# The moving operands of the dense products begin 96 bytes past a multiple of 128 in their partition

## The chip, the cores and the metric

The program runs on one core of one Trainium2 chip. A time is the time that the device takes for one execution, in microseconds (us). The kernel before takes 1717.57 us, the median of 3 runs (1716.57 to 1721.44). The profile was taken in an execution of its own.

## The reference

Two transformer-like blocks on 256 tokens of 1024 channels, all in float32. The first block: a parallel mixer (forgetting attention beside a causal convolution of width 31), cross attention to a memory of 256 tokens, and a mixture of 32 experts. The second block has two layers, each with two feed-forward networks (FFNs) and a mixer between them.

```python
def swiglu(h, w13, w2):
    gate, up = jnp.split(h @ w13, 2, axis=-1)      # 1024 -> 2 x 2816
    return (jax.nn.silu(gate) * up) @ w2           # 2816 -> 1024

for l in range(2):
    if l == 1:
        k_shared, v_shared = shared_kv(x, kv_norm, w_kv, k_norm)
    x = x + 0.5 * swiglu(rms_norm(x, ffn1_norm[l]), ffn1_w13[l], ffn1_w2[l])
    h = rms_norm(x, mix_norm[l])
    x = x + (rglru_block(h, ...) if l == 0 else stick_breaking_block(h, k_shared, v_shared, ...))
    x = x + 0.5 * swiglu(rms_norm(x, ffn2_norm[l]), ffn2_w13[l], ffn2_w2[l])
```

The four FFNs are the greater part of the time outside the experts.

## The kernel before, in words

**The dense products.** Activations lie with channels on the 128 partitions and the 256 tokens along the free dimension. Float32 accuracy comes from splitting each operand into a high and a low part of type fp32r and adding three matmuls (`mm3`, lines 177 to 179): w-high by x-high (L177), w-high by x-low (L178), w-low by x-high (L179). In each, the 128 x 128 slice of a weight tile `wh` or `wl` is loaded into the array (the stationary operand), and a 128 x 256 slice of an activation tile is streamed through it (the moving operand). The activation tiles are

- `xgh`, `xgl`: the input of a stage, 8 chunks of 256 tokens, read by `proj2` (line 195) in 2 x 8 x 3 = 48 matmuls for each weight tile;
- `hh`, `hl`: one hidden pair of an FFN, 2 chunks, two buffers, read by `rowproj` in 8 x 2 x 3 = 48 matmuls for each weight tile;
- `qT`/`kT` and `zp`/`v` (the mixer's output product), `cath`/`catl` (the memory attention's), `yh`/`yl` (the recurrent block's), `xkvh`/`xkvl` (the stick-breaking block's), read in the same way.

In `product` (line 1174) the roles are turned round: the weights stream, and `xg`, `xkv` or `cat` slices are loaded.

**An FFN** (`ffn`, line 1059) has 11 steps j. Each computes a gate block (48 matmuls into PSUM tile `A`), an up block (48 into `B`), and, from j = 1 to 9, a step of the second product for the pair before (48 matmuls into `acc`). Two pairs are left for the tail, 96 matmuls in which the two weight tiles alternate. Each block takes one weight tile of 1 MB, which a DMA loads, ACT rounds to `wh` (L157) and DVE subtracts to `wl` (L158); three `wh`/`wl` slots rotate.

**Places in memory.** Every pool hands out its tiles one after another in the order of their first request, each rounded up to 32 bytes. Where a tile begins in its partition is therefore decided by what was requested before it. The pool `x` holds `xgh` and `xgl` and nothing else; `first`, `moe` and `second` follow it and take turns in the same space; `rglru` and `attn` lie behind `second`.

**The experts** (from 257 us to 710 us) read float32 weights by DMA into `raw`, `wh`, `wl` and `xgh`/`xgl`, used there as a ring of 16 buffers, and multiply them without splitting (L941, L967).

Of the kernel before, what the change touches and what calls it, by code (L numbers as in the profile page):

```python
# [8 lines left out]
F32 = mybir.dt.float32  # L9
F32R = mybir.dt.float32r  # L10
I32 = mybir.dt.int32
# [5 lines left out]
P = 128  # L17
T = 256
# [29 lines left out]
class Block:  # L48
    def __init__(s, ctx, tc, io):
        s.tc, s.nc, s.ctx, s.io = tc, tc.nc, ctx, io  # L50
        s.n = s.turn = s.place = 0
        s.queue = None
        pool = lambda name, bufs, **k: ctx.enter_context(tc.tile_pool(name=name, bufs=bufs, **k))
        s.cp = pool("const", 1)
        s.wp = pool("weights", 3)
        s.tp = pool("temps", 2)
        s.xp = pool("x", 1)
        s.pa = pool("acc", 1, space=PSUM)
        s.pp = pool("ps", 2, space=PSUM)

# [32 lines left out]
    def col(s, name, c=0, n=1):  # L93
        o = PCOL[name] + c
        return s.par[:, o:o + n]

    def pair(s, pool, C, tag, bufs=None, N=T):
        return (s.new(pool, [P, C, N], tag + "h", F32R, bufs), s.new(pool, [P, C, N], tag + "l", F32R, bufs))
# [126 lines left out]
    def rsqrt(s, x, n):  # L225

        nc = s.nc
        xh = s.tmp([P, n], f"nr{n}", 6 if n > 4 else 8)
        nc.vector.tensor_scalar_mul(xh, x, -0.5)
        yi = s.tmp([P, n], f"nr{n}", 6 if n > 4 else 8).bitcast(I32)  # L230
        nc.vector.tensor_single_scalar(yi, x.bitcast(I32), 1, op=ALU.arith_shift_right)
        y = s.tmp([P, n], f"nr{n}", 6 if n > 4 else 8)
        nc.vector.tensor_scalar(y.bitcast(I32), yi, -1.0, float(0x5F3759DF), op0=ALU.mult, op1=ALU.add)
        u = s.tmp([P, n], f"nr{n}", 6 if n > 4 else 8)
        for _ in range(3):
            if n == 2:
                for i in range(n):
                    c = slice(i, i + 1)
                    nc.vector.scalar_tensor_tensor(u[:, c], y[:, c], xh[:, c], y[:, c], op0=ALU.mult, op1=ALU.mult)
            else:  # L240
                nc.vector.tensor_mul(u, y, y)
                nc.vector.tensor_mul(u, u, xh)
            nc.vector.scalar_tensor_tensor(y, u, 1.5, y, op0=ALU.add, op1=ALU.mult)
        return y
# [779 lines left out]
    def after_moe(s, acc, p2):  # L1024


        nc = s.nc
        gg = s.new(p2, [P, KC], "gg")
        nc.vector.tensor_mul(gg, s.col("final_g", 0, 8), s.col("ffn1_norm_2", 0, 8))

        g2 = s.tmp([P, 2 * KC], "nr16", 6).rearrange("p (k n) -> p k n", n=2)
        nc.vector.memset(g2, 1.0)
        nc.vector.tensor_mul(g2[:, :, 1], s.col("final_g", 0, 8), s.col("final_g", 0, 8))
        xg = s.pair(s.xp, KC, "xg")
        st = s.sums_pe(g2)
        for b in range(4):
            s.update(acc[b], b, 1.0, xg, gg, st)
        got = {}

        def rows(what):  # L1040
            if not got:


                x = s.tmp([P, 4], "nr4", 8)
                pb = s.bank()[0]
                nc.vector.tensor_scalar_mul(x.rearrange("p (n h) -> p n h", h=2), st["pe"].rearrange("p h n -> p n h"), 1.0 / D)
                nc.vector.tensor_scalar_add(x[:, 0:2], x[:, 0:2], EPS)
                nc.vector.scalar_tensor_tensor(x[:, 2:4], x[:, 0:2], EPS, x[:, 2:4], op0=ALU.mult, op1=ALU.add)
                y = s.rsqrt(x, 4)
                got["r"] = s.spread(y[:, 2:4], pb)  # L1050
                got["r1"] = s.spread(y[:, 0:2], pb, s.tmp([P, T]))
            return got[what]

        def rescale():
            for k in range(KC):
                nc.vector.scalar_tensor_tensor(s.xT[:, k], s.xT[:, k], s.col("final_g", k), rows("r1"), op0=ALU.mult, op1=ALU.mult)
        return xg, rows, rescale

    def ffn(s, pf, xg, rows, w13, w2, g, extra=None, between=None):

        nc = s.nc
        J = F // 256
        step, tail = s.rowproj(w2, 2 * J)
        held = []
        for j in range(J):
            pg, pu = s.ps([P, 2, T], "A"), s.ps([P, 2, T], "B")
            w = s.wload(w13[j], KC, 256)
            s.proj2(pg, w, xg, late=2 if j == 0 else 0)
            w = s.wload(w13[J + j], KC, 256)
            s.proj2(pu, w, xg)  # L1070
            rb2 = bc(rows("r"), [P, 2, T], 1)
            tg, tu = s.tmp([P, 2, T], "gs", 2), s.tmp([P, 2, T], "us", 2)
            nc.vector.tensor_mul(tg, pg, rb2)
            nc.scalar.activation(tg, tg, AF.Silu)
            nc.vector.tensor_mul(tu, pu, rb2)
            nc.vector.tensor_mul(tu, tu, tg)
            hl = s.pair(pf, 2, "h", 2)
            s.split(hl, slice(0, 2), tu)
            held.append((j, hl))
            if 0 < j < J - 1:  # L1080
                step(*held.pop(0))
            if j == 4 and between is not None:
                between()
        if g is None:
            outv = s.io["out"].rearrange("(c p) t -> p c t", p=P)

            def done(ps, b):
                s.update(ps, b, 0.5, None, None, None)
                nc.sync.dma_start(outv[:, 2 * b:2 * b + 2], s.xT[:, 2 * b:2 * b + 2])
            tail(held, done)  # L1090
            return None
        xg, st, done = s.residual(0.5, g)

        def done2(ps, b):
            done(ps, b)
            if extra is not None:
                for m in (2 * b, 2 * b + 1):
                    s.split(extra[0], m, s.xT[:, m], extra[1][:, m:m + 1])
        tail(held, done2)
        return xg, s.rows(st)  # L1100

    def rglru(s, pr, xg, rows, g):
# [7 lines left out]
        def branch(col, dst, late=0):  # L1110
            w = s.wload(io["a_w_in_2"][col // 256], KC, 256)
            ps = s.ps([P, 2, T])
            s.proj2(ps, w, xg, late=late)
            nc.vector.tensor_mul(dst, ps, bc(rows("r"), [P, 2, T], 1))
# [186 lines left out]
    def run(s):  # L1301
        tc, io = s.tc, s.io
        s.setup()
        with tc.tile_pool(name="first", bufs=1) as p1:
            s.cur = p1
            xg, rows, km, vm = s.mixer(p1)
            xg, st = s.mem_attention(p1, xg, rows, km, vm)
        with tc.tile_pool(name="moe", bufs=1) as mt:
            acc = s.moe(mt, xg, st)
        with tc.tile_pool(name="second", bufs=1) as p2:  # L1310
            s.cur = p2
            xg, rows, rescale = s.after_moe(acc, p2)
            gains = lambda name, l: s.col(name, 8 * l, 8)
            ffn = lambda xg, rows, n, l, g, *more: s.ffn(
                p2, xg, rows, io[f"ffn{n}_w13_2"][l], io[f"ffn{n}_w2_2"][l], g, *more)
            xg, rows = ffn(xg, rows, 1, 0, gains("mix_norm_2", 0), None, rescale)
            with tc.tile_pool(name="rglru", bufs=1) as pr:
                xg, rows = s.rglru(pr, xg, rows, gains("ffn2_norm_2", 0))
            with tc.tile_pool(name="attn", bufs=1) as pk:
                xkv = s.pair(pk, KC, "xkv")  # L1320
                xg, rows = ffn(xg, rows, 2, 0, gains("ffn1_norm_2", 1), (xkv, gains("kv_norm_2", 0)))
                kT, vA = s.shared_kv(pk, xkv, rows)
                xg, rows = ffn(xg, rows, 1, 1, gains("mix_norm_2", 1))
                xg, rows = s.stick(pk, xg, rows, kT, vA, gains("ffn2_norm_2", 1))
            ffn(xg, rows, 2, 1, None)
# [76 lines left out]
```

## Time and profile before

| | |
|---|---|
| median of 3 runs | 1717.57 us |
| the profiled execution | 1718.19 us, of it 1716.4 us span |
| TensorE matmul busy (PE) | 1659.7 us, 97% of the span |
| weight loads (PEld) | 1349.5 us, beside the matmuls |
| VectorE (DVE), ScalarE (ACT) | 922.9 us, 704.0 us |
| TensorE clock granted | 0.984 of full speed in the mean |
| DMA | 408.03 MB |

PE is TensorE, "x" is a count of instructions, and L177 is a line of the kernel. Matmuls are pipelined: one is shown with some 280 ns, but in a dense stretch the next begins some 115 ns after it. How fast the stream runs is therefore read from starts: the start of one block of 48 less the start of the block before it, divided by 48.

### The profile page before, as it was taken

Reading aid. Unit: us, or ns where it says so; the run is one execution under the profiler, and the core shown is the slowest. Engines: PE = TensorE matmul, PEld = TensorE weight load, DVE = VectorE, ACT = ScalarE, POOL = GpSimd, SP = SyncE. Lnnn points to the kernel's source line nnn. Section 1 sums busy time; section 2 is a strip of 40 time slices with the busy share of each in tenths; the row PEclk is TensorE's granted clock in tenths of the full one; section 3 lists DMA queues with packets and bytes.
Section 4 is the critical chain, followed back from the end, with each engine's and each line's share of the span. In section 5 each row is a group of like instructions: output and inputs, shape, how many; then the busy total and the mean of one; then the engine's idle time right before and its main releaser. Section 6 shows DMA issues by size and latency. Waiting matters only on the chain.

```text
span 1716.4 us, 28131 instructions
## 1 busy us (share of the span) xinstructions
PE 1659.7 (97%) x11883; PEld 1349.5 (79%) x11883; DVE 922.9 (54%) x1618; ACT 704.0 (41%) x1138; POOL 5.0 (0%) x19
## 2 busy tenths in 40 slices
PE   8999989999999998699999999999999999999998
PEld 7878984444444443299999999999899997689998
DVE  7998741111111110265657886556755558876554
ACT  8526532111111111244445754445644446764442
POOL 0000000000000000000000000000000000000000
PEclk9999989999999999889999999999999999899999
DMA  9334359999999999845553555554555454044530
GB/s 367 132 120 175 142 226 367 419 419 420 419 419 419 420 419 420 361 183 191 197 184 136 197 221 172 197 184 161 198 196 197 174 195 172 25 148 172 197 123 26
DMA packets 60227, 408.03 MB, mean 238 GB/s; under 512 B 6592, under 2 KB 9920, under 8 KB 11456
## 3 DMA queue, kind: packets, MB, share of 16 engines
q1 hardware_dynamic: 60096, 406.18, 61.4%
q8 instruction: 95, 1.56, 0.4%
q14 instruction: 36, 0.29, 0.0%
HBM read 405.11 MB, written 1.05 MB: 237 GB/s over the span
## 4 chain that ended last, share of the span: by engine, by line
PE 54%; DVE 2%; ACT 1%; issue 1%; DMA 0%; SPq 0%; ACTq 0%; DVEq 0%
PE A L179 6%; PE A L178 6%; PE A L177 6%; PE acc L177 5%; PE acc L178 5%; PE B L177 5%; PE B L178 5%; PE acc L179 5%; PE B L179 5%; ACT wh L157 1%; PE A L1262 1%; DVE wl L158 1%; PE A L967 1%; PE B L416 0%; PE B L408 0%
## 5 line engine op out<-in xcount | busy, mean ns | idle before, releaser
L157 ACT CAST wh<-raw 128x1024 fp32r<-128x1024 f32 (+2 forms) x378 | 378.0, 1034 | 445.0 <-issue 363.8
L158 DVE TENSOR_TENSOR wl<-raw,wh 128x1024 fp32r<-128x1024 f32 (+2 forms) x378 | 448.6, 1204 | 160.5 <-ACT wh L157 159.7
L177 PE MATMUL B<-xgh,wh 128*128 128x256 f32 x872 | 246.1, 282 | 6.9 <-ACT wh L157 6.9
L177 PE MATMUL A<-xgh,wh 128*128 128x256 f32 (+1 forms) x872 | 246.7, 283 | 0.0
L179 PE MATMUL A<-xgh,wl 128*128 128x256 f32 (+1 forms) x872 | 245.5, 282 | 0.1
L178 PE MATMUL A<-xgl,wh 128*128 128x256 f32 (+1 forms) x872 | 245.5, 282 | 0.1
L179 PE MATMUL B<-xgh,wl 128*128 128x256 f32 x872 | 245.6, 282 | 0.0
L178 PE MATMUL B<-xgl,wh 128*128 128x256 f32 x872 | 245.2, 281 | 0.0
L178 PE MATMUL acc<-hl,wh 128*128 128x256 f32 x704 | 194.7, 278 | 0.2
L179 PE MATMUL acc<-hh,wl 128*128 128x256 f32 x704 | 194.5, 277 | 0.0
L177 PE MATMUL acc<-hh,wh 128*128 128x256 f32 x704 | 193.1, 278 | 0.5 <-ACT hh L218 0.5
L177 PEld LDWEIGHTS B<-xgh,wh 128*128 128x128 f32 x872 | 164.5, 189 | 7.9 <-ACT wh L157 7.2
L179 PEld LDWEIGHTS B<-xgh,wl 128*128 128x128 f32 x872 | 164.4, 189 | 1.5 <-DVE wl L158 1.0
L178 PEld LDWEIGHTS A<-xgl,wh 128*128 128x128 f32 (+1 forms) x872 | 164.7, 189 | 0.6 <-DVE xgl L222 0.4
L177 PEld LDWEIGHTS A<-xgh,wh 128*128 128x128 f32 (+1 forms) x872 | 164.8, 189 | 0.3
L179 PEld LDWEIGHTS A<-xgh,wl 128*128 128x128 f32 (+1 forms) x872 | 164.7, 189 | 0.4 <-DVE wl L158 0.3
L178 PEld LDWEIGHTS B<-xgl,wh 128*128 128x128 f32 x872 | 164.7, 189 | 0.5 <-DVE xgl L222 0.2
L852 DVE COPY gx<-B 128x128 f32<-128x128 f32 x64 | 18.6, 291 | 231.9 <-PE B L846 223.6
L941 PE MATMUL A<-raw,gx 128*64 128x512 f32 x560 | 130.1, 603 | 8.6 <-DMA raw<-in_w_gu_dram 6.2
L178 PEld LDWEIGHTS acc<-hl,wh 128*128 128x128 f32 x704 | 132.1, 188 | 0.6 <-DVE hl L219 0.6
L179 PEld LDWEIGHTS acc<-hh,wl 128*128 128x128 f32 x704 | 132.2, 188 | 0.0
L177 PEld LDWEIGHTS acc<-hh,wh 128*128 128x128 f32 x704 | 130.9, 188 | 1.2 <-ACT hh L218 1.1
(407 smaller groups left out, 2422.4 us busy)
## 6 DMA issues: line engine op xcount, KB each, us to landing
raw<-in_ffn_w_dram SPq DMA_DIRECT2D x132, 1024.0 KB, 4.8
raw<-in_w_gu_dram SPq DMA_DIRECT2D x70, 1024.0 KB, 19.9
raw<-in_w_down_dram SPq DMA_DIRECT2D x34, 1024.0 KB, 19.9
wh<-in_w_gu_dram SPq DMA_DIRECT2D x22, 1024.0 KB, 19.9
wl<-in_w_gu_dram SPq DMA_DIRECT2D x22, 1024.0 KB, 19.9
wh<-in_w_down_dram SPq DMA_DIRECT2D x11, 1024.0 KB, 19.9
wl<-in_w_down_dram SPq DMA_DIRECT2D x11, 1024.0 KB, 19.9
raw<-in_a_w_in_dram SPq DMA_DIRECT2D x8, 1024.0 KB, 5.0
```

Source lines behind the costliest of these rows:

```text
L157: nc.scalar.copy(wh[:, lo:hi], raw[:, lo:hi])
L158: nc.vector.tensor_sub(wl[:, lo:hi], raw[:, lo:hi], wh[:, lo:hi].bitcast(F32))
L177: mm(out, w[0], x[0], start=first, stop=False)
L178: mm(out, w[0], x[1], start=False, stop=False)
L179: mm(out, w[1], x[0], start=False, stop=last)
L852: nc.vector.tensor_copy(dst, pg[:, :, i])
L941: s.pe(s.nc.tensor.matmul(ps[g * CAP:(g + 1) * CAP], gx[t // 2][:, 2 * (t % 2) + c], w[:, g, c * 512:c * 512 + 512], start=t + c == 0, sto ...
L967: s.pe(nc.tensor.matmul(pd[n * CAP:(n + 1) * CAP], hx[:, 2 * t + c], w[:, c, n * 512:n * 512 + 512], start=t + c == 0, stop=t + c == 2))
L1262: mm(sc[:, lo:lo + ke], qT[b:b + 64, c, qb * P:qb * P + P], kT[b:b + 64, c, 0:ke], start=True, stop=True)
```

## The change

A tile of 32 bytes (`pad`) is requested in the pool `x` ahead of `xgh`. A new helper `lay` requests tiles by tag and size ahead of their use, so that they get the first places of a pool: the mixer's and the memory attention's product tiles in `first`, `hh` and `hl` in `second`, `yh` and `yl` in `rglru`. A tile `pad` of 64 bytes stands behind `hl`, and the buffers `nr4` (16 bytes each, asked for only by the norm behind the experts) are 5 in place of 8, so that what follows comes to 96 as well.

```diff
@@ Block.__init__
         s.xp = pool("x", 1)
+        s.new(s.xp, [P, 8], "pad")
@@ Block
+    def lay(s, pool, *tiles):
+        for tag, n, bufs in tiles:
+            for _ in range(bufs):
+                s.new(pool, [P, n // 4], tag, F32, bufs)
@@ rsqrt (four such lines) and after_moe (one)
-        xh = s.tmp([P, n], f"nr{n}", 6 if n > 4 else 8)
+        xh = s.tmp([P, n], f"nr{n}", 6 if n > 4 else 5 if n == 4 else 8)
...
-                x = s.tmp([P, 4], "nr4", 8)
+                x = s.tmp([P, 4], "nr4", 5)
@@ run
+            s.lay(p1, ("cath", 8192, 1), ("catl", 8192, 1), ("v", 4096, 1), ("qT", 4096, 1), ("kT", 4096, 1), ("zp", 4 * (30 + T) * 4, 1))
             xg, rows, km, vm = s.mixer(p1)
...
+            s.lay(p2, ("hh", 2048, 2), ("hl", 2048, 2), ("pad", 64, 1))
             xg, rows, rescale = s.after_moe(acc, p2)
...
+                s.lay(pr, ("yh", 8192, 1), ("yl", 8192, 1))
                 xg, rows = s.rglru(pr, xg, rows, gains("ffn2_norm_2", 0))
```

The built programs hold the same instructions on every engine, in the same order and with the same waits on the same semaphore values; what differs is where tiles begin. In bytes from the start of the partition:

| tile | before | past 128 | after | past 128 |
|---|---|---|---|---|
| `xgh`, `xgl` | 138816, 147008 | 64 | 138848, 147040 | 96 |
| `hh` (two), `hl` (two) | 163680, 165728, 167776, 169824 | 96 | 155232, 157280, 159328, 161376 | 96 |
| `xkvh`, `xkvl` | 171872, 180064 | 96 | the same | 96 |
| `yh`, `yl` of the recurrent block | 212928, 221120 | 64 | 171872, 180064 | 96 |
| `cath`, `catl` | 172064, 219712 | 32, 64 | 155232, 163424 | 96 |
| `qT`, `kT`, `v`, `zp` of the mixer | 195136, 199232, 186944, 155200 | 64 | 175712, 179808, 171616, 183904 | 96 |
| `wh` (three), `wl` (three) | 77344 to 93728, 101920 to 118304 | 32 | the same | 32 |
| `raw` (eight) | 11808 to 69152 | 32 | the same | 32 |
| expert tiles (`oh`, `gx`, `oT`, `hx`, ...) | | 0 | each 32 further | 32 |

The slices of all these tiles that a dense product reads begin at multiples of 512 bytes from the tile's start, so each has its tile's place past 128.

## Rows read from the trace of the kernel before

**Rows 1.** The page's part 1, TensorE's and VectorE's busy time.
```profile
PE 1659.7 (97%) x11883; PEld 1349.5 (79%) x11883; DVE 922.9 (54%) x1618; ACT 704.0 (41%) x1138; POOL 5.0 (0%) x19
```

**Rows 2.** Windows: the mixer, the four FFNs with their neighbours, and experts.
```profile
core 0: us, PE busy (x) PEld busy (x) DVE busy (x) ACT busy (x) POOL busy (x), PEclk, DMA share, GB/s
30.00:170.00 140.00, 136.42 (x839) 117.28 (x838) 125.22 (x306) 70.83 (x136) 1.83 (x2) 1.00 0.45 169
742.00:930.00 188.00, 187.84 (x1593) 187.35 (x1593) 116.26 (x151) 80.32 (x101) 0.00 (x0) 0.99 0.46 163
1010.00:1200.00 190.00, 189.59 (x1613) 188.05 (x1612) 120.81 (x154) 88.78 (x115) 0.00 (x0) 1.00 0.52 183
1243.00:1433.00 190.00, 189.84 (x1613) 188.64 (x1612) 114.02 (x129) 85.55 (x109) 0.96 (x3) 1.00 0.52 183
1523.00:1716.00 193.00, 188.61 (x1599) 187.36 (x1597) 113.73 (x141) 79.80 (x99) 0.00 (x0) 1.00 0.37 132
400.00:560.00 160.00, 158.52 (x930) 71.70 (x928) 26.19 (x66) 28.99 (x71) 0.00 (x0) 1.00 1.01 419
```

**Rows 3.** Groups of TensorE by shape: busy us, mean ns, idle before.
```profile
L177 PE MATMUL A<-xgh,wh 128*128 128x256 f32 x864 | 244.4, 283 | 0.0
...
L178 PE MATMUL acc<-hl,wh 128*128 128x256 f32 x704 | 194.7, 278 | 0.2
```

**Rows 4.** Timeline of TensorE, first FFN: the first matmul of seven blocks.
```profile
start us, us, engine line op out<-in xcount [idle before <-releaser]
...
765.59 0.28 PE L177 MATMUL acc<-hh,wh 128*128 128x256 f32 x1
...
771.24 0.28 PE L177 MATMUL A<-xgh,wh 128*128 128x256 f32 x1
...
777.00 0.28 PE L177 MATMUL B<-xgh,wh 128*128 128x256 f32 x1
...
782.76 0.28 PE L177 MATMUL acc<-hh,wh 128*128 128x256 f32 x1
...
788.20 0.28 PE L177 MATMUL A<-xgh,wh 128*128 128x256 f32 x1
...
793.81 0.28 PE L177 MATMUL B<-xgh,wh 128*128 128x256 f32 x1
...
799.41 0.28 PE L177 MATMUL acc<-hh,wh 128*128 128x256 f32 x1
```

**Rows 5.** Timeline of TensorE, fourth FFN: the first matmul of four blocks.
```profile
1582.27 0.28 PE L177 MATMUL acc<-hh,wh 128*128 128x256 f32 x1
...
1587.93 0.28 PE L177 MATMUL A<-xgh,wh 128*128 128x256 f32 x1
...
1593.53 0.28 PE L177 MATMUL B<-xgh,wh 128*128 128x256 f32 x1
...
1599.13 0.28 PE L177 MATMUL acc<-hh,wh 128*128 128x256 f32 x1
```

**Rows 6.** Timeline of TensorE, the first FFN's tail and one later wait.
```profile
915.99 0.28 PE L177 MATMUL acc<-hh,wh 128*128 128x256 f32 x1
...
918.25 0.28 PE L179 MATMUL acc<-hh,wl 128*128 128x256 f32 x1
918.69 0.73 PE L177 MATMUL acc<-hh,wh 128*128 128x256 f32 x4 [0.16 <-ACT hh L218]
919.26 0.28 PE L178 MATMUL acc<-hl,wh 128*128 128x256 f32 x1
...
927.63 0.28 PE L177 MATMUL B<-xgh,wh 128*128 128x256 f32 x1
...
1549.27 0.28 PE L179 MATMUL acc<-hh,wl 128*128 128x256 f32 x1
...
1554.34 0.28 PE L178 MATMUL A<-xgl,wh 128*128 128x256 f32 x1
```

**Rows 7.** Timeline of TensorE, the recurrent block's output product, first matmul and its successor.
```profile
987.54 0.28 PE L177 MATMUL acc<-yh,wh 128*128 128x256 f32 x1
...
1010.33 0.28 PE L177 MATMUL A<-xgh,wh 128*128 128x256 f32 x1
```

More of the change, by code (lines that the diff above doesn't have):

```diff
@@ L227, in rsqrt @@
         nc = s.nc
-        xh = s.tmp([P, n], f"nr{n}", 6 if n > 4 else 8)
+        xh = s.tmp([P, n], f"nr{n}", 6 if n > 4 else 5 if n == 4 else 8)
         nc.vector.tensor_scalar_mul(xh, x, -0.5)
-        yi = s.tmp([P, n], f"nr{n}", 6 if n > 4 else 8).bitcast(I32)
+        yi = s.tmp([P, n], f"nr{n}", 6 if n > 4 else 5 if n == 4 else 8).bitcast(I32)
         nc.vector.tensor_single_scalar(yi, x.bitcast(I32), 1, op=ALU.arith_shift_right)
-        y = s.tmp([P, n], f"nr{n}", 6 if n > 4 else 8)
+        y = s.tmp([P, n], f"nr{n}", 6 if n > 4 else 5 if n == 4 else 8)
         nc.vector.tensor_scalar(y.bitcast(I32), yi, -1.0, float(0x5F3759DF), op0=ALU.mult, op1=ALU.add)
-        u = s.tmp([P, n], f"nr{n}", 6 if n > 4 else 8)
+        u = s.tmp([P, n], f"nr{n}", 6 if n > 4 else 5 if n == 4 else 8)
         for _ in range(3):
```

## The prediction

> **What bounds the kernel now.** I read the page's busy times first: TensorE is busy for 97% of the span, VectorE for 54% [rows 1]. Then the windows: in the four FFN stretches PE is busy for 187.84 of 188, 189.59 of 190, 189.84 of 190 and 188.61 of 193 us at full clock, while DVE and ACT have a third of their time left and the DMA queues half of theirs [rows 2]. Nothing is to be seen there but TensorE's own pace. In the experts the DMA engines are full (share 1.01, 419 GB/s), so that stage goes by bytes [rows 2]. The change moves no instruction and no wait; what it can alter is how long one matmul takes, and it tells on the end wherever PE is the bound.
>
> So the pace of the stream is what has to be read. The groups of PE already show a difference: matmuls on `xg` have a mean of 283 ns, those on `hh`/`hl` 278 ns [rows 3]. Since these overlap, I take the timeline and divide blocks of 48 by their starts.
>
> - `hh` block, 782.76 to 788.20: 5.44 us, 113.3 ns a matmul [rows 4].
> - `xg` blocks, 788.20 to 793.81 and to 799.41: 5.61 and 5.60 us, 116.8 ns [rows 4].
>
> `hh` begins 96 past 128 and `xg` 64 past. That is the case for the change. But the same rows hold two things against it. The `hh` block of 765.59 to 771.24 takes 5.65 us, 117.7 ns, on the same tiles [rows 4], and in the fourth FFN the `hh` block from 1582.27 to 1587.93 takes 5.66 us, with its `xg` blocks at 5.60 [rows 5]. So 96 has two paces, 113.3 and 117.8 ns, and each holds through a whole block. Of the 36 step blocks of the four FFNs, 24 run at 113.3 (8 in each of the first three FFNs) and 12 at 117.8 (the first step of each of the three, and all nine of the fourth); one block at 113.3 and two at 117.8 stand in the rows [rows 4, 5].
>
> **When 96 is quick.** The tail of the first FFN shows it within one product. From 915.99 to 918.25 its first 20 matmuls follow the `xg` blocks without a gap: 2.26 / 20 = 113 ns. Then PE waits for ACT (0.16 us), and from 919.26 to 927.63 the other 71 take 8.37 / 71 = 117.9 ns, on the same tiles and weight slots, to the end [rows 6]. I find 15 stretches on tiles at 96 that begin behind a wait or gap, in the tails, the stick-breaking block and the first steps; their means are 117.5 to 118 ns, and 116.8 for one of five matmuls. The first is that tail and the next to last is the first step of the fourth FFN, 1549.27 to 1554.34, 43 matmuls in 5.07 us, 117.9 ns [rows 6]. The quick pace was entered only straight from an `xg` block at 64, and once lost it did not come back within a block. The pace is thus a state that the stream carries with it, and a wait puts it into the slow one.
>
> **The change part by part.** It removes and adds no instruction. Its terms are the streams that change place, and the neighbours that had their pace from them. With every moving tile at 96, no stream at 64 is left from which the quick pace is entered. Each FFN begins with waits for its weights and norms, so I take the slow pace, 5.655 us a block (5.65 and 5.66 measured), as the likeliest for all of them.
>
> 1. `hh` steps that are quick now: 24 x (5.655 - 5.44) = +5.2 us; the first 20 matmuls of three tails: 3 x 20 x 4.5 ns = +0.3 us.
> 2. `xg` blocks of the FFNs, 4 x 22 = 88. Some 78 run at 5.605 now: +0.05 each, +3.9 us. Four run at 5.76 (771.24 to 777.00 and to 782.76 [rows 4], and the two at the same place of the third FFN): -0.1 each, -0.4 us. Some six in first steps run at 5.65 already: 0. Together +3.5 us.
> 3. `xg` blocks of the other stages, 20 of them: +0.05 each, +1.0; in the mixer PE is idle for 3.6 of 140 us and DVE is busy for 125 [rows 2], so part of that is hidden. I take +0.7 us; without any cover it is 1.0.
> 4. `yh`/`yl`: 192 matmuls from 987.54 to 1010.33, 22.79 us, 118.7 ns [rows 7]; at 117.8 they take 22.62: -0.2 us. The mixer's and the memory attention's product tiles: nothing either way, 0.5 us at most.
> 5. Expert tiles move by 32 too. They lie beside a full DMA [rows 2]; zero, and the same for DMA into `xg`, which is two of 16 ring buffers (`raw` at 32 and `xg` at 64 are filled alike in the same stage). The other tiles that ACT and DVE use only wait for PE in the FFNs.
>
> The sum is +5.5 + 3.5 + 0.7 - 0.2 = +9.5 us on an execution of 1718.19, 1727.7. The profiled execution is 0.6 us over the median, so against the median it is 1727.
>
> Bounds of the unknown. No tile of the trace has both the new place and a start without a gap behind 96, so the pace of the whole stream is bounded by the paces seen: 113.3 ns [rows 4] below and 120 ns (5.76 us, [rows 4]) above. At 120 the 88 FFN `xg` blocks alone would cost 84 x 0.155 = +13 us and the 36 steps +24 x 0.32 + 12 x 0.105 = +9 us; only tiles at 64 showed that pace, so I give it little. The lower end is the first rival.
>
> [...]
>
> **The rivals.**
>
> *The quick pace everywhere.* The step blocks that follow `xg` at once are quick in three FFNs of four; if what decides is that all operands have one place, the slow pace has nothing to feed it. Against it: the 15 starts behind waits. Its price: 78 + 6 + 4 FFN `xg` blocks, 78 x -0.165 - 6 x 0.21 - 4 x 0.32 = -15.4; 20 others, -3.3, of which I count -2.7; 12 slow steps x -0.215 = -2.6; four tails, 76 x 4.5 ns each, -1.3; `yh` -1.0, the mixer's, memory's and stick-breaking block's products -2.2. Together -25 us: 1692.
>
> *Stage by stage.* Each FFN falls into one of the two paces. For two of four quick: about -9 and +4: 1710 to 1714, between the others.
>
> *The place past 128 is not what counts.* `yh` lies 64 past 128 as `xg` does and runs at 118.7 against 116.8 ns [rows 4, 7]. So something wider than 128 bytes enters, and then `hh`, which moves by 8448 bytes, and `xg` may come to a third pace. At `xg`'s present 5.605 us for everything the 24 quick steps lose 0.165 each, +4.0 us, the other 12 and the tails gain 1 us: 1720 to 1721. If only the steps stay as they are: 1718.
>
> **How the numbers follow.** Chances: slow pace after waits (forecast) 0.42; quick everywhere 0.30; stage by stage 0.10; another pace or no effect 0.18. About 0.3%, 5 us, is what a measurement of this kernel can tell from no change. Faster: 0.30 + 0.08 = 0.38. Within: 0.02 + 0.15 = 0.17. Slower: 0.42 + 0.03 = 0.45. The forecast's own range is 1722 to 1731 (steps alone, or a little of the 120 pace). Since both signs hold much, the range is 1690 to 1730.
>
> **What would show it.** In the changed kernel's timeline the step blocks of the first three FFNs from 782 us on should take 5.65 in place of 5.44 us and the gate and up blocks 5.65 in place of 5.61; the mean of both groups should come together near 280 ns; the experts should last as long as before. The forecast is wrong if gate and up blocks take 5.44 us, which is the first rival, or if a block takes a time that no block has now, which is the third.

## The result, and the profile after

The changed kernel takes 1727.97 us, the median of 5 runs (1726.53 to 1729.51), beside 1717.95 us (1716.57 to 1721.62) for the kernel before on the same chip: ratio 1.0051, 95% interval [1.0036, 1.0067]. It is slower by half a per cent. The forecast was 1727 us. The profiled execution has a span of 1726.2 us, 9.8 us more than that of before.

First the page's busy times after, to be laid beside [rows 1].

```profile
PE 1667.9 (97%) x11883; PEld 1360.0 (79%) x11883; DVE 922.7 (53%) x1618; ACT 704.1 (41%) x1138; POOL 5.0 (0%) x19
```

The counts of instructions are those of before and the times of VectorE and ScalarE too, to 0.2 us; TensorE has 8.2 us more. The windows after are the stretches of [rows 2]: us, then busy us and instructions of each engine, granted clock, DMA share, GB/s.

```profile
core 0: us, PE busy (x) PEld busy (x) DVE busy (x) ACT busy (x) POOL busy (x), PEclk, DMA share, GB/s
30.00:170.00 140.00, 136.49 (x839) 117.40 (x838) 125.20 (x306) 71.53 (x137) 1.83 (x2) 1.00 0.46 169
742.00:930.00 188.00, 187.94 (x1568) 187.63 (x1567) 112.50 (x142) 77.01 (x94) 0.00 (x0) 0.98 0.47 163
...
1243.00:1433.00 190.00, 189.94 (x1587) 188.33 (x1586) 107.99 (x112) 81.04 (x96) 0.00 (x0) 1.00 0.53 186
...
400.00:560.00 160.00, 157.57 (x920) 71.05 (x922) 26.12 (x66) 29.03 (x71) 0.00 (x0) 1.00 1.01 420
```

PE is as full as before, but 1568 matmuls fit into the 188 us of the first FFN where 1593 did, and 1587 in place of 1613 into those of the third. The experts still stand at a DMA share of 1.01. The pace is read from the starts of blocks, in the timeline of TensorE after, first FFN, from the step block that answers to the first of [rows 4]. L184 to L186 are now the three matmuls of `mm3`; in the kernels of the experiments the numbers shift by a line.

```profile
767.04 0.28 PE L184 MATMUL acc<-hh,wh 128*128 128x256 f32 x1
...
772.69 0.28 PE L184 MATMUL A<-xgh,wh 128*128 128x256 f32 x1
...
778.35 0.28 PE L184 MATMUL B<-xgh,wh 128*128 128x256 f32 x1
...
784.00 0.28 PE L184 MATMUL acc<-hh,wh 128*128 128x256 f32 x1
...
789.65 0.28 PE L184 MATMUL A<-xgh,wh 128*128 128x256 f32 x1
...
795.30 0.28 PE L184 MATMUL B<-xgh,wh 128*128 128x256 f32 x1
```

Every block now takes 5.65 or 5.66 us, 117.8 ns a matmul: the `hh` block of 784.00 to 789.65 where that of before took 5.44, and the `xg` blocks where they took 5.61 and, behind the first step, 5.76 [rows 4]. The fourth FFN and the recurrent block's output product after, which answer to [rows 5, 7]:

```profile
991.53 0.28 PE L184 MATMUL acc<-yh,wh 128*128 128x256 f32 x1
...
1014.14 0.28 PE L184 MATMUL A<-xgh,wh 128*128 128x256 f32 x1
...
1591.35 0.28 PE L184 MATMUL acc<-hh,wh 128*128 128x256 f32 x1
...
1597.01 0.28 PE L184 MATMUL A<-xgh,wh 128*128 128x256 f32 x1
...
1602.66 0.28 PE L184 MATMUL B<-xgh,wh 128*128 128x256 f32 x1
```

`yh` takes 22.61 us for 192, 117.8 ns, and the fourth FFN's blocks 5.66 and 5.65. There are two exceptions in the whole trace, both blocks of 48 on `xg` that stand shortly behind a stretch with waits; this is the later one, in the fourth FFN's first step.

```profile
1551.42 0.28 PE L184 MATMUL B<-xgh,wh 128*128 128x256 f32 x1
...
1556.86 0.62 PE L184 MATMUL acc<-hh,wh 128*128 128x256 f32 x4
1557.31 0.28 PE L184 MATMUL A<-xgh,wh 128*128 128x256 f32 x1
1557.92 0.39 PE L185 MATMUL acc<-hl,wh 128*128 128x256 f32 x1 [0.33 <-DVE hl L226]
```

1551.42 to 1556.86 is 5.44 us, 113.3 ns. Five matmuls later PE waits 0.33 us for `hl`, and from 1557.92 on the stream is back at 117.8. So a stream in which all places are 96 can run at 113.3, but it rarely comes to that.

### The profile page after: what moved, and what is told of

It is laid out like the page before. It is cut to its first block, busy times and chain, and to the rows that moved or that the text cites. A ratio compares the mean times of both kernels' runs of the same rounds, so it can differ in the third digit from the quotient of the medians.

```text
span 1726.2 us, 28131 instructions
## 1 busy us (share of the span) xinstructions
PE 1667.9 (97%) x11883; PEld 1360.0 (79%) x11883; DVE 922.7 (53%) x1618; ACT 704.1 (41%) x1138; POOL 5.0 (0%) x19
## 4 chain that ended last, share of the span: by engine, by line
PE 54%; DVE 2%; ACT 1%; issue 1%; DMA 0%; SPq 0%; ACTq 0%; DVEq 0%
PE A L185 6%; PE A L186 6%; PE A L184 6%; PE acc L185 6%; PE acc L184 6%; PE acc L186 5%; PE B L185 5%; PE B L184 5%; PE B L186 5%; ACT wh L164 1%; PE A L1269 1%; DVE wl L165 1%; PE A L974 0%; PE B L423 0%; PE B L415 0%
## 5 line engine op out<-in xcount | busy, mean ns | idle before, releaser
L184 PE MATMUL B<-xgh,wh 128*128 128x256 f32 x872 | 246.4, 283 | 6.4 <-ACT wh L164 6.4
L184 PE MATMUL A<-xgh,wh 128*128 128x256 f32 (+1 forms) x872 | 246.8, 283 | 0.0
L186 PE MATMUL B<-xgh,wl 128*128 128x256 f32 x872 | 246.1, 282 | 0.0
L186 PE MATMUL A<-xgh,wl 128*128 128x256 f32 (+1 forms) x872 | 245.7, 282 | 0.1
L186 PE MATMUL acc<-hh,wl 128*128 128x256 f32 x704 | 195.8, 279 | 0.0
L184 PE MATMUL acc<-hh,wh 128*128 128x256 f32 x704 | 194.2, 280 | 0.2
L184 PEld LDWEIGHTS B<-xgh,wh 128*128 128x128 f32 x872 | 164.9, 189 | 7.3 <-ACT wh L164 6.7
L186 PEld LDWEIGHTS B<-xgh,wl 128*128 128x128 f32 x872 | 164.6, 189 | 1.5 <-DVE wl L165 0.9
L184 PEld LDWEIGHTS A<-xgh,wh 128*128 128x128 f32 (+1 forms) x872 | 165.0, 189 | 0.3
L186 PEld LDWEIGHTS A<-xgh,wl 128*128 128x128 f32 (+1 forms) x872 | 164.5, 189 | 0.4 <-DVE wl L165 0.3
L948 PE MATMUL A<-raw,gx 128*64 128x512 f32 x560 | 127.9, 595 | 8.7 <-DMA raw<-in_w_gu_dram 6.3
L186 PEld LDWEIGHTS acc<-hh,wl 128*128 128x128 f32 x704 | 131.9, 187 | 0.0
L184 PEld LDWEIGHTS acc<-hh,wh 128*128 128x128 f32 x704 | 130.9, 188 | 0.9 <-ACT hh L225 0.8
```

Of the source, the lines that this page charges most:

```text
L184: mm(out, w[0], x[0], start=first, stop=False)
L186: mm(out, w[1], x[0], start=False, stop=last)
L948: s.pe(s.nc.tensor.matmul(ps[g * CAP:(g + 1) * CAP], gx[t // 2][:, 2 * (t % 2) + c], w[:, g, c * 512:c * 512 + 512], start=t + c == 0, sto ...
```

## Experiments

All kernels are the changed kernel with tiles shifted by other pads; "at 64" means 64 bytes past a multiple of 128. The quick pace is 113.3 ns a matmul, and a block is said to open it when the blocks behind it run at that pace and those ahead of it did not. The first four ran on one chip, beside 1720.28 us for the kernel before. Ratios are to the kernel before on the same chip, paces are means of the starts in the profiled execution.

**xg back at 64, the rest at 96.** This is the first half of the change undone.

```diff
-        s.new(s.xp, [P, 8], "pad")
-            s.lay(p1, ("cath", 8192, 1), ...
+            s.lay(p1, ("pad0", 32, 1), ("cath", 8192, 1), ...
-            s.lay(p2, ("hh", 2048, 2), ("hl", 2048, 2), ("pad", 64, 1))
+            s.lay(p2, ("pad0", 32, 1), ("hh", 2048, 2), ("hl", 2048, 2), ("pad", 64, 1))
```

> The changed kernel with xgh and xgl back at 64 past 128 (138816, 147008); hh, hl and all other product tiles stay where the change put them, at 96. Theory A (the pace of a stream at 96 is a state: a wait leaves it in the 117.8 ns pace, entering it straight from blocks at 64 can put it in the 113.3 ns pace): step blocks of hh are quick again in most places (5.44 us, about 24 of 36), gate and up blocks 5.61 us, time 1717 to 1719 us. Rival B (hh lost its quick pace because it moved by 8448 bytes): steps stay at 5.65 us, gate and up blocks 5.61 us, time 1722 to 1724 us.

Measured: 1720.93 us, ratio 1.0005 [0.9993, 1.0017]. The whole loss is gone, though `hh` stays where the change put it. 31 of the 36 step blocks run at 113.4 ns (24 before), the fourth FFN's among them. Its timeline shows where the quick pace begins: the second block of `xg` behind a step at 117.8, the step after it, the next block.

```profile
1567.48 0.28 PE L183 MATMUL B<-xgh,wh 128*128 128x256 f32 x1
...
1573.24 0.28 PE L183 MATMUL acc<-hh,wh 128*128 128x256 f32 x1
...
1578.68 0.28 PE L183 MATMUL A<-xgh,wh 128*128 128x256 f32 x1
```

The `xg` block takes 5.76 us, 120.0 ns; the `hh` block behind it 5.44, 113.3 ns. So `xg` at 64 is what fed the quick pace before.

**hh and hl at 64, the rest at 96.** The roles of `xg` and `hh` changed round.

```diff
-            s.lay(p2, ("hh", 2048, 2), ("hl", 2048, 2), ("pad", 64, 1))
+            s.lay(p2, ("gg", 32, 1), ("nr4", 16, 5), ("pad0", 32, 1), ("hh", 2048, 2), ("hl", 2048, 2), ("pad", 32, 1))
```

> The changed kernel with hh and hl at 64 past 128 (155456 and on) and everything else at 96. Theory A: now the gate block follows a block at 64 without a wait, so gate and up blocks from j = 2 on can become quick (5.44 us, up to 72 of 88), the steps take 5.60 to 5.76 us: 1728 - 72 x 0.215 = 1712 us, 1710 to 1716. Rival B (the quick pace belongs to the old place of hh, or entry does not matter): gate and up blocks stay at 5.65 us, time 1725 to 1729 us.

Measured: 1712.41 us (1705.33 to 1717.93), ratio 0.9954 [0.9935, 0.9972]: faster than both kernels. Timeline of its third FFN, four steps of which the second shows the opening:

```profile
1264.49 0.28 PE L184 MATMUL acc<-hh,wh 128*128 128x256 f32 x1
...
1270.09 0.28 PE L184 MATMUL A<-xgh,wh 128*128 128x256 f32 x1
...
1281.40 0.28 PE L184 MATMUL acc<-hh,wh 128*128 128x256 f32 x1
...
1287.15 0.28 PE L184 MATMUL A<-xgh,wh 128*128 128x256 f32 x1
...
1292.60 0.28 PE L184 MATMUL B<-xgh,wh 128*128 128x256 f32 x1
...
1298.04 0.28 PE L184 MATMUL acc<-hh,wh 128*128 128x256 f32 x1
```

A step at 5.60 us (116.7 ns) doesn't help: two `xg` blocks follow in 11.31 us, 117.8 ns. The next step takes 5.75 us (119.8), and from there on `xg` takes 5.45 and 5.44 us, to the FFN's end. In the fourth FFN of this execution no step came to 120, and its `xg` stayed at 117.8.

**All streamed tiles at 64.** The pad in the pool `x` alone is left out (`-        s.new(s.xp, [P, 8], "pad")`).

> The changed kernel without the 32-byte pad in the pool x: every product tile at 64 past 128. Theory A: a stream at 64 settles at 116.7 ns, blocks 5.60 us everywhere, steps too; against the kernel before the 24 quick steps lose 0.165 us each, the 12 others gain 0.05, the four blocks at 5.76 us gain 0.15: 1720 to 1722 us. Rival: the other pace seen at 64, 120 ns (5.76 us), takes the stream: 1735 to 1738 us.

Measured: 1724.15 us, ratio 1.0020 [1.0008, 1.0031]. Blocks run at 116.6 to 116.8 ns in three FFNs and at 117.8 in nearly all of the fourth. So one place for all, be it 96 or 64, doesn't make the stream quick.

**The weights 32 further on, the streamed tiles as in the changed kernel.** The 32 bytes stand ahead of `raw`, `wh` and `wl`, which come to 64; no streamed tile moves.

```diff
         s.wp = pool("weights", 3)
+        s.new(s.wp, [P, 8], "wpad", F32, 1)
-        s.new(s.xp, [P, 8], "pad")
```

> All moving tiles exactly where the changed kernel has them, but raw, wh and wl 32 bytes further, at 64 past 128 (the 32-byte pad stands ahead of them instead of ahead of xg). If only the moving operand's place counts: blocks 5.65 us, 1726 to 1729 us, as the changed kernel. If the place of moving and loaded operand to each other counts (now 32 apart, as xg and wh were before): gate and up blocks 5.60 to 5.61 us, time 1718 to 1722 us or another pace altogether.

Measured: 1720.58 us, ratio 1.0003 [0.9993, 1.0013]. Timeline of its first FFN, three blocks:

```profile
770.68 0.28 PE L184 MATMUL A<-xgh,wh 128*128 128x256 f32 x1
...
776.28 0.28 PE L184 MATMUL B<-xgh,wh 128*128 128x256 f32 x1
...
781.88 0.28 PE L184 MATMUL acc<-hh,wh 128*128 128x256 f32 x1
```

5.60 us, 116.7 ns, with `xg` and `hh` at the very addresses at which they take 5.65 in the changed kernel. The place of the operand that is loaded counts too, not only that of the one that streams. In the fourth FFN of this kernel the blocks take 5.65 us all the same, as with all streamed tiles at 64.

The next four ran beside 1721.16 us for the kernel before. Their texts call R the theory that the distance from the loaded to the streamed operand decides, taken modulo 64, and S the theory that it is the streamed tile's own place.

**hh and hl at 0.**

```diff
-            s.lay(p2, ("hh", 2048, 2), ("hl", 2048, 2), ("pad", 64, 1))
+            s.lay(p2, ("pad0", 32, 1), ("hh", 2048, 2), ("hl", 2048, 2), ("pad", 32, 1))
```

> The changed kernel with hh and hl at 0 past 128 (155264 and on), 96 from the loaded weights' place (32), everything else at 96. Theory R (what counts is the place of the moving operand to that of the loaded one, modulo 64: 0 gives the paces 113.3 and 117.8 ns, 32 gives 116.7, 117.8 and 120, and the quick pace is entered from a block of the other kind): as with hh at 64, steps 5.60 to 5.63 us, gate and up blocks 5.44 us in the first three FFNs, ratio to the kernel before 0.994 to 0.998, about 1712 us. Rival S (modulo 128, so 0 is a place of its own): steps take another time than any block so far, or gate and up blocks stay at 5.65 us, ratio 1.003 or more.

Measured: 1733.60 us, ratio 1.0067 [1.0050, 1.0084]. `hh` runs at 119.9 ns and `xg` at 117.8. R with modulus 64 misses.

**hh and hl at 32**, the place of the weights.

```diff
-            s.lay(p2, ("hh", 2048, 2), ("hl", 2048, 2), ("pad", 64, 1))
+            s.lay(p2, ("gg", 32, 1), ("nr4", 16, 5), ("hh", 2048, 2), ("hl", 2048, 2), ("pad", 64, 1))
```

> The changed kernel with hh and hl at 32 past 128 (155424 and on), the same place as the loaded weights, everything else at 96. Theory R: 32 is the same kind as 96, so no block gives an entry: all blocks 5.65 us, ratio to the kernel before 1.004 to 1.007, 1727 us. Rival S: steps at a pace of their own (the memory attention's product at 32 and 64 ran at 117 to 120 ns before), gate and up blocks may become quick: ratio 0.995 to 1.000.

Measured: 1732.21 us, ratio 1.0058 [1.0041, 1.0075]; `hh` at 120.0 ns, `xg` at 117.8. R's ratio is met, but not its blocks: the steps take 5.76 us, not 5.65. Here, as with `hh` at 0, `hh` stands at 120 all the time and opens nothing, so it is not the 120 ns alone that opened the quick pace above.

**All streamed tiles at 0** (`[P, 8]` of the pad in `x` becomes `[P, 16]`).

> Every product tile at 0 past 128 (pad of 64 bytes in the pool x). Theory R: the same kind as all at 64: blocks 5.60 us, some stages at 5.65, ratio 1.001 to 1.004, 1722 to 1726 us. Rival S: an operand that begins on a multiple of 128 streams best: blocks 5.44 us or less everywhere, ratio 0.985 to 0.990, 1692 to 1700 us.

Measured: 1744.59 us, ratio 1.0127 [1.0109, 1.0144], the longest of all. Both theories missed it. Timeline, first FFN, two blocks of 5.76 us, 120.0 ns:

```profile
773.56 0.28 PE L184 MATMUL A<-xgh,wh 128*128 128x256 f32 x1
...
779.32 0.28 PE L184 MATMUL B<-xgh,wh 128*128 128x256 f32 x1
...
785.08 0.28 PE L184 MATMUL acc<-hh,wh 128*128 128x256 f32 x1
```

**Weights and streamed tiles together 64 on.** Weights at 96, `xg`, `hh` and `cath` at 32, the distance between them as in the changed kernel up to 128; `yh` and `xkv` at 0.

```diff
         s.wp = pool("weights", 3)
+        s.new(s.wp, [P, 16], "wpad", F32, 1)
-            s.lay(p2, ("hh", 2048, 2), ("hl", 2048, 2), ("pad", 64, 1))
+            s.lay(p2, ("hh", 2048, 2), ("hl", 2048, 2), ("pad", 32, 1))
```

> raw, wh and wl at 96 past 128 (64 bytes further) and the moving tiles xg, hh, hl and the first stage's at 32: the same 64 bytes between them as in the changed kernel, at other places (yh and xkv come to 0). Theory R: blocks 5.65 us as in the changed kernel, but for the few behind yh and xkv that may be quick: ratio 1.002 to 1.007, 1722 to 1729 us. Rival (the absolute place of the moving operand counts): the paces of 96 are not seen, blocks near 5.60 or 5.76 us.

Measured: 1725.20 us, ratio 1.0022 [1.0010, 1.0034]. Timeline: two blocks of the first FFN, and the product on `yh`.

```profile
770.16 0.28 PE L185 MATMUL A<-xgh,wh 128*128 128x256 f32 x1
...
775.82 0.28 PE L185 MATMUL B<-xgh,wh 128*128 128x256 f32 x1
...
781.47 0.28 PE L185 MATMUL acc<-hh,wh 128*128 128x256 f32 x1
...
989.00 0.28 PE L185 MATMUL acc<-yh,wh 128*128 128x256 f32 x1
...
1011.40 0.28 PE L185 MATMUL A<-xgh,wh 128*128 128x256 f32 x1
```

`xg` takes 5.66 and 5.65 us as in the changed kernel, at another place but the same distance; `yh`, whose distance is 0 - 96 = 32 modulo 128, takes 22.40 / 192 = 116.7 ns, as `xg` did before. 47 matmuls on `cath` even run at 113.4 from 217.13 us on. R's ratio is met here too, but R takes the distances 0 and 64 for alike, and 32 and 96, which the runs above refute: 120.0 ns at 0 and 117.8 at 64, 116.7 at 32 and 119.9 at 96. So it is the distance, and a modulus of 64 is too small. The distance modulo 128 is theory D of the last four runs; whether it is 128 or 256 is taken up at the end. Of these four the first three ran beside 1719.85 us, the last beside 1720.19 us.

**High parts at 96, low parts at 64**, and the mirror of it. If a stretch at 64 opens the quick pace, perhaps every third matmul does.

```diff
-        s.new(s.xp, [P, 8], "pad")
+        s.lay(s.xp, ("xgl", 8192, 1), ("pad", 32, 1), ("xgh", 8192, 1))
-            s.lay(p2, ("hh", 2048, 2), ("hl", 2048, 2), ("pad", 64, 1))
+            s.lay(p2, ("gg", 32, 1), ("nr4", 16, 5), ("pad0", 32, 1), ("hl", 2048, 2), ("pad", 32, 1), ("hh", 2048, 2))
```

> The high parts xgh and hh stay at 96 past a multiple of 128, the low parts xgl and hl begin at 64 (some 7300 matmuls, two on a high part for each on a low part). Weights at 32 as in the changed kernel. Theory D (what decides is the distance from the loaded to the streamed operand modulo 128, and a stretch at distance 32 brings the stream at distance 64 into the quick pace): each low matmul opens the quick pace again, 113.3 for the high ones and 116.7 for the low ones, 114.4 ns in the mean, 7300 x 3.4 ns = 25 us less than the changed kernel, ratio to the kernel before 0.988 to 0.993. Rival E (the quick pace is entered only from a whole block at distance 32, each matmul otherwise has the pace of its distance): 117.8 and 116.7, 117.4 in the mean, ratio 1.002 to 1.004. Rival F (a change of distance between neighbours costs something of its own): 120 ns and more, ratio above 1.010.

> The mirror of the kernel with high parts at 96 and low parts at 64: xgh and hh at 64, xgl and hl at 96. Theory D: 116.7 for the high parts and 113.3 for the low ones, 115.6 ns in the mean, 7300 x 2.2 = 16 us less than the changed kernel, ratio 0.994 to 0.998. Rival E: 116.7 and 117.8, 117.1 in the mean, ratio 1.001 to 1.003. Rival F: 120 ns and more, ratio above 1.010.

Measured: 1730.58 us, ratio 1.0057 [1.0037, 1.0077], and for the mirror (`xgl` and `xgh`, `hl` and `hh` exchanged in both lines) 1727.43 us, 1.0049 [1.0034, 1.0065]. Blocks run at 117.6 to 117.9 ns in both. The idea fell, and none of the three expectations has the number: a stream whose distance alternates between 64 and 32 runs near 117.8, and no single matmul opens anything.

**Weights at 96, xg, hh and cath at 64.** The place that `xg` had before, at the distance 64 - 96 = 96 modulo 128.

```diff
         s.wp = pool("weights", 3)
+        s.new(s.wp, [P, 16], "wpad", F32, 1)
-        s.new(s.xp, [P, 8], "pad")
+        s.new(s.xp, [P, 16], "pad")
-            s.lay(p2, ("hh", 2048, 2), ("hl", 2048, 2), ("pad", 64, 1))
+            s.lay(p2, ("hh", 2048, 2), ("hl", 2048, 2))
```

> Weights begin at 96, xg, hh and cath at 64, where the kernel before has xg; yh and xkv at 0. Theory D (the distance from loaded to streamed operand modulo 128): 64 less 96 is 96 modulo 128, the distance of the kernel with all streamed tiles at 0, so 120 ns for the xg and hh blocks and 116.7 for yh and xkv (distance 32), ratio 1.010 to 1.014. Rival (the place of the streamed tile itself): 116.7 for xg and hh as in the kernel with all of them at 64, ratio 1.000 to 1.003.

Measured: 1740.53 us, ratio 1.0121 [1.0103, 1.0138]. Timeline, first FFN:

```profile
772.65 0.28 PE L185 MATMUL A<-xgh,wh 128*128 128x256 f32 x1
...
778.41 0.28 PE L185 MATMUL B<-xgh,wh 128*128 128x256 f32 x1
...
784.17 0.28 PE L185 MATMUL acc<-hh,wh 128*128 128x256 f32 x1
```

5.76 us, 120.0 ns, for the tiles that take 5.60 at this place when the weights are at 32; `yh` at 0 runs at 116.7. The distance decides; the place of the streamed tile by itself doesn't.

**One hidden buffer at 64, the other at 96.** The kernel with `hh` at 64, but half as many stretches at the other distance; the edit is shown against that kernel.

```diff
-            hl = s.pair(pf, 2, "h", 2)
+            hl = s.pair(pf, 2, "h%d" % (j % 2), 1)
-        mask = s.new(s.cur, [P, 384], "hl", F32, 2)
+        mask = s.new(s.cur, [P, 384], "h1l", F32, 1)
-            e = s.new(s.cur, [P, 384], ("hh", "hl")[h % 2], F32, 2)
+            e = s.new(s.cur, [P, 384], ("h0h", "h0l", "h1h")[h % 3], F32, 1)
-... ("pad0", 32, 1), ("hh", 2048, 2), ("hl", 2048, 2), ("pad", 32, 1))
+... ("pad0", 32, 1), ("h0h", 2048, 1), ("h0l", 2048, 1), ("pad", 32, 1), ("h1h", 2048, 1), ("h1l", 2048, 1))
```

> As the kernel with hh and hl at 64, but the two hidden buffers apart: steps of even j at 64, steps of odd j at 96; xg and all else at 96, weights at 32. In every FFN six blocks in succession (288 matmuls) are then at distance 64, and one of 48 at distance 32. If the pace is a state that the stream at distance 64 keeps over any number of blocks while PE doesn't wait, and that a whole block at distance 32 can open: after the opening gate, up and odd step blocks run at 113.3 to 113.4 ns and even steps at 117.0; in three FFNs of four this saves four or five odd steps x 48 x 3.5 ns = 0.8 us each, 2 to 3 us in all, ratio 0.992 to 0.996. Rival: with half as many blocks at 64 the opening comes later or not at all; then gate and up blocks stay at 117.8 in some more of the FFNs (4.7 us each), ratio 0.997 to 1.004.

Measured: 1710.49 us (1704.58 to 1718.38), ratio 0.9940 [0.9917, 0.9964]. Its fourth FFN changes pace in the middle:

```profile
1605.90 0.28 PE L184 MATMUL B<-xgh,wh 128*128 128x256 f32 x1
...
1611.55 0.28 PE L184 MATMUL acc<-h0h,wh 128*128 128x256 f32 x1
...
1617.31 0.28 PE L184 MATMUL A<-xgh,wh 128*128 128x256 f32 x1
...
1622.76 0.28 PE L184 MATMUL B<-xgh,wh 128*128 128x256 f32 x1
...
1628.19 0.28 PE L184 MATMUL acc<-h1h,wh 128*128 128x256 f32 x1
...
1633.63 0.28 PE L184 MATMUL A<-xgh,wh 128*128 128x256 f32 x1
```

Up block 5.65 us, step on the buffer at 64 5.76 us, and then 5.45, 5.43, 5.44: the quick pace, over `xg` and the buffer at 96 alike. In this execution the first FFN never opened, the second and third did early. The number met the first expectation; the mechanism did so in three FFNs, and the fear of the rival came true in the first. Against the kernel with all of `hh` at 64 the intervals overlap, so which of the two is better is open.

## Why the prediction was right

- *TensorE's pace is the bound.* It held: the windows of the FFNs are as full as before, those of the first and third hold fewer matmuls (1568 in place of 1593, 1587 in place of 1613), and the experts stayed at a DMA share of 1.01.
- *The quick steps lose their feeder (term 1, +5.2 and +0.3).* From start to start, matmul by matmul against the kernel before, the 2101 that can be compared on `hh` and `hl` cost 5.25 us more. That `xg` at 64 was the feeder was argued from one tail; the run with `xg` alone put back shows it.
- *The xg blocks come to 5.65 (terms 2 and 3, +3.5 and +0.7).* The 5093 on `xg` cost 3.81 us more, 0.4 less than the 4.2 forecast.
- *yh gains 0.2, the other products nothing (term 4).* -0.18 us and +0.15. *The experts are free (term 5)*: they are, with 470.3 us before and 469.6 after from the first of their matmuls on L941 (L948 after) to the end of the last on L967 (L974).
- *What the sum left out.* Starts behind gaps and waits, which stood in no term, cost 1.3 us more in all, over half of that ahead of the experts. All together are 10.3 us from the first to the last such matmul, and the span grew by 9.8; the sum was 9.5. It came so near because misses of -0.25 us on `hh` and -0.4 on `xg` pull against the 1.3 of the waits, and because the first such matmul starts 0.5 us earlier after the change; that is luck.
- *A wait puts the stream into the slow pace, and the quick one is entered only from a block at 64.* Too strong. Two blocks of the changed kernel came to 113.3 shortly behind waits, and even next to a block at 64 the entry mostly fails (below). It was enough for the sign and the size, since little more than those two blocks came to the quick pace in the changed kernel.
- *That 96 past 128 is what counts.* Wrong as it stood, and without harm here because `wh` and `wl` kept their place. The third rival suspected it, because `yh` before is 64 past 128 as `xg` is and ran at 118.7 [rows 7]. Its price didn't come, but its reason, that something wider than 128 bytes enters, is not refuted (see the end).
- *120 ns only at 64.* Wrong: `hh` at 32 ran at 120.0 ns (distance 0), and `hh` at 0 and all streamed tiles at 0 at 119.9 and 120.0 (distance 96).
- *What would show it.* The blocks did so. The groups' means did not: `A<-xgh` stays at 283 ns and `hl` rises from 278 to 280, so they did not come together. Overlapping durations were the wrong view for it; starts were the right one.
- *No effect.* Places that are all multiples of 32 are not alike: the same matmuls at such places span ratios from 0.9940 (half of `hh` at 64) to 1.0127 (all streamed tiles at 0).

## What to carry to other kernels

Where TensorE is the bound, as it is here in the FFNs, work out the distance from each loaded operand to each streamed one modulo 256, of which the runs cover 0, 32, 64 and 96, and one stream 160, and read the pace of the stream from starts of blocks, not from the mean duration of a matmul. For this shape distances 0 and 96 were the worst (120.0 and 119.9 ns a matmul); 32 and 64 were better (116.7 and 117.8), and a stream that is mostly at 64 with blocks at 32 between them was the best (113.3 once opened, ratios 0.9954 and 0.9940). Making all places alike, which looks tidy, took away the very neighbours from which the quick pace began (ratio 1.0051). Other shapes were not compared.

## What the runs showed of the hardware

Pace of the dense streams (128 x 128 loaded, 256 columns streamed, fp32r) by the distance of the streamed from the loaded operand modulo 128 (the granted clock was 1.00 in the third FFN before, after, and with `hh` or half of it at 64, and 0.981 to 0.987 in the mean of each execution):

| distance | places streamed / loaded | ns a matmul |
|---|---|---|
| 64 | 96 / 32, 32 / 96 | 117.8; 113.3 once opened |
| 32 | 64 / 32, 96 / 64, 0 / 96 | 116.7 (116.9 beside the quick pace); at times 117.8 or 120.0 |
| 96 | 0 / 32, 64 / 96 | 119.9, 120.0 |
| 0 | 32 / 32 | 120.0 |

The table says modulo 128, but the runs do not tell 128 from 256. All dense streams of this shape in the fourteen programs have the same distance modulo 256 as modulo 128, but for one: `yh` before begins at 212928 and the loaded tiles at 77344, so it stands at 32 modulo 128 and at 160 modulo 256. It is also the odd one in pace. Rows 7 give 22.79 us for its 192 matmuls; the 97th, in the same timeline of the kernel before, cuts them into halves of 11.40 and 11.39 us, so the pace of 118.7 ns holds throughout.

```profile
998.94 0.28 PE L177 MATMUL acc<-yh,wh 128*128 128x256 f32 x1
```

No other stretch of 24 or more of these matmuls without a gap, in any of the fourteen traces, has a mean between 118.1 and 119.4 ns. `yh` at 32 by both counts runs at 116.7 (weights 32 further on) or at 117.8 (all at 64). It is one stream of one kernel, and no run was made for it, so this stays open; 256 fits all that was measured, and 512 isn't needed (after the change `xg` stands at 64 and `yh` at 320 modulo 512, both at 117.8).

The pace is a state that passes from block to block. In the profiled executions of the kernel before, of the one with `xg` at 64 and of the two with `hh` or half of it at 64, a stretch at distance 32 goes over into one at 64 without a gap, with 12 matmuls or more on either side, 134 times. Where the stretch at 64 ahead of it was quick, the next one was quick too, 89 times of 89. Where it was not, it depended on the pace of the stretch at 32 between: at 120 ns the quick pace followed 8 times of 8, at 117 4 times of 33, at 118 not once in 4. Why distance 32 falls into one or the other of its paces, and which waits open the quick one, stays open. So does why the runs of the two kernels with `hh` at 64 spread over 13 and 14 us; that the FFNs opened at different times in different executions would do it, but each has only one profile.
